# A chunked state-space scan on one core: its chunks taken in pairs, with two buffers each for B, inputs and decayed inputs

## The chip, the core and the metric

The kernel runs on one core of a Trainium2 chip. The metric is device time in microseconds (us) of one execution, the median of several; lower is better. The engines are TensorE (PE in the profile, with its weight loads as PEld), VectorE (DVE), ScalarE (ACT), GpSimd (POOL) and the queue engine SyncE (SP). Each engine takes its own instructions strictly in the order in which they were written down for it, and they wait for one another through semaphores.

## What is computed

One layer of a hybrid decoder in float32: a layer norm, a wide projection, a convolution branch (31 taps) beside a Mamba-2 state-space branch, a gated sum, an output projection, and a convolutional feed-forward part. The change touches only the chunked state-space scan. Cut to that, the reference is:

```python
# 1024 steps, chunks of L = 128; 4 groups g of 8 heads r, head size p = 64, state n = 128
a_cs  = cumsum(dt * a_head)                          # inside a chunk
decay = tril(exp(a_cs[l] - a_cs[s]))
cb     = einsum("bclgn,bcsgn->bcgls", C, B)
y_diag = einsum("bcgrls,bcsgrp->bclgrp", cb * decay, x * dt)
states = einsum("bclgn,bcgrl,bclgrp->bcgrpn", B, exp(a_cs[-1] - a_cs), x * dt)
carry  = exp(a_cs[-1]) * carry + states              # from chunk to chunk
y_off  = einsum("bclgn,bcgrpn,bcgrl->bclgrp", C, carry_before, exp(a_cs))
y      = y_diag + y_off
```

## The kernel before

The sequence is worked through in two halves of 512 steps (`hh` 0 and 1). In each half `mixers` runs four groups of heads (`g` 0 to 3). For a group it projects B, C and x (`column`, `conv4`) and the convolution branch (`glu`), calls `ssd_group`, which goes over the four chunks of 128 steps in that half, and then writes the 31-tap convolution `conv31` (30 VectorE instructions of 128x512 for each of two tiles) at low priority. `combine` follows: it reads the convolution back, averages over channels (the sum `mean` on POOL, its split `avgm`, and the matmul at L757), and multiplies with the next weights. The second half of the kernel is the feed-forward part, which the change does not touch.

Nearly all of TensorE's work is the split-precision projection `mm3` (L175, L176, L177): three 128x512 matmuls for each weight block. In the prediction "a projection matmul" is one of these. Every weight block is loaded by SP, rounded by ACT (L141) and its rest is formed by VectorE (L142) before TensorE can use it, in three rotating buffers.

For each chunk `ssd_group` has these parts:

- **transposes** of x and B (L570, L573) and the product of C and B (L574), into two PSUM banks (`px`, `pb`) of the four-bank pool "sm";
- a load of the cumulative sums `m` (L580, 512 KB, issued by POOL, two buffers), eight Relu (L585) and one Exp (L589) on ACT, and the masking product `m * cbm` (L601) on VectorE;
- `xs` (L593) on VectorE, the copy `bt` (L577) and the decayed inputs `xsd` (L600, eight instructions) on ACT;
- **carried** (L606): four matmuls of the state with C, and the product at L607;
- **masked** (L610): eight matmuls, one for each head. Each uses 64 of the array's 128 columns, even heads the lower and odd heads the upper half;
- **update** (L620): one 128x512 matmul that makes the new state. An explicit order keeps it behind the chunk's masked products (`tc.issue_after`, L619). L624 and L627 then update the state on VectorE, and L631 adds the masked products to the result.

Plain float32 matmuls (all of these) are two records each in the profile, the transposes one. `bt`, `xs` and `xsd` have one buffer. The order on each engine comes from a scheduler that lists instructions by priority, when its own timeline has their inputs ready; projections of later weights are put between the parts of a chunk.

Of the kernel before, what the change touches and what calls it, by code (L numbers as in the profile page):

```python
# [54 lines left out]
def kernel(  # L55
# [322 lines left out]
    def time_steps(pl, hh, ps):  # L378

        n2 = 2 * HEADS  # L380
        dtc = pl.tile([n2, HALF], F32, tag="yo", bufs=2, name=f"dtc{hh}")
        A.activation(
            out=dtc, in_=ps[:n2, :], func=AF.Identity, bias=pc[:n2, PC_DTB : PC_DTB + 1]
        )
        pt = bank(0)
        for c in range(4):
            TE.transpose(pt[:, c * n2 : (c + 1) * n2], dtc[:, c * P : (c + 1) * P], ident[:n2, :n2])
        n = 4 * HEADS
        dtv, wds = (d.rearrange("p c h -> p (c h)") for d in dts)
        work = pl.tile([P, 8 * P], F32, tag="m", bufs=2, name=f"sp{hh}")  # L390
        v, s, s2, q, a = (work[:, i * n : (i + 1) * n] for i in range(5))
        ea = work[:, 5 * n : 6 * n + HEADS]
        e = ea[:, :n]
        V.tensor_scalar_mul(ea[:, n:], a_log, -1.0)
        pv = pt[:, : 2 * n].rearrange("p (c i h) -> p c i h", c=4, i=2)
        vv = v.rearrange("p (c h) -> p c h", c=4)
        V.tensor_copy(vv, pv[:, :, 0, :])
        V.tensor_tensor(out=vv, in0=vv, in1=pv[:, :, 1, :], op=ALU.add)
        A.activation(out=e, in_=v, func=AF.Abs)
        A.activation(out=ea, in_=ea, func=AF.Exp, scale=-1.0)  # L400
        V.tensor_scalar_add(s, e, 2.0)
        V.reciprocal(out=s, in_=s)
        V.tensor_mul(s, s, e)
        V.tensor_mul(s2, s, s)
        V.tensor_scalar(
            out=q, in0=s2, scalar1=1.0 / 17.0, scalar2=1.0 / 15.0, op0=ALU.mult, op1=ALU.add
        )
        for k in (13, 11, 9, 7, 5, 3):
            V.tensor_mul(q, q, s2)
            V.tensor_scalar_add(q, q, 1.0 / k)  # L410
        V.tensor_mul(q, q, s2)
        V.scalar_tensor_tensor(out=q, in0=q, scalar=1.0, in1=s, op0=ALU.add, op1=ALU.mult)
        V.tensor_scalar_max(v, v, 0.0)
        V.scalar_tensor_tensor(out=dtv, in0=q, scalar=2.0, in1=v, op0=ALU.mult, op1=ALU.add)
        V.scalar_tensor_tensor(
            out=a.rearrange("p (c h) -> p c h", c=4),
            in0=dts[0],
            scalar=-1.0,
            in1=ea[:, n:].unsqueeze(1).to_broadcast([P, 4, HEADS]),
            op0=ALU.mult,  # L420
            op1=ALU.mult,
        )
        pa = bank(0)
        for c in range(4):
            hs = slice(c * HEADS, (c + 1) * HEADS)
            TE.matmul(pa[hs, :P], a[:, hs], upper, start=True, stop=True)
        eh = pl.tile([P, HALF], F32, tag="yo", bufs=2, name=f"sp_eh{hh}")[:, :P]
        cum = pl.tile([P, HALF], F32, tag="xsd", name=f"sp_cum{hh}")[:, :P]
        A.activation(out=eh, in_=pa[:, :P], func=AF.Exp)
        V.tensor_copy(cum, pa[:, :P])  # L430
        G.dma_start(cum_scr[hh].rearrange("c h l -> (c h) l"), cum)
        for c in range(4):
            G.dma_start(e_scr[hh][:, c * P : (c + 1) * P], eh[c * HEADS : (c + 1) * HEADS])
        pc_t = bank(0)
        TE.transpose(pc_t[:, :P], cum, ident)
        V.tensor_copy(cums.rearrange("p c h -> p (c h)"), pc_t[:, :n])
        pe = bank(0)
        for i, m in enumerate((later, ones)):
            TE.matmul(pe[:, i * n : (i + 1) * n], m, a, start=True, stop=True)
        ev = edc.rearrange("p i c h -> p (i c h)")  # L440
        A.activation(out=ev, in_=pe[:, : 2 * n], func=AF.Exp)
        V.tensor_mul(wds, dtv, edc[:, 0].rearrange("p c h -> p (c h)"))
# [103 lines left out]
    def ssd_group(pl, hh, g, xT, BT, CT, gate):  # L546
# [13 lines left out]
        def by_tile(t):  # L560
            return t.rearrange("p (i t) -> p i t", i=4)

        for c in range(4):
            nm = f"{hh}_{g}_{c}"
            cs = slice(c * P, (c + 1) * P)
            first = hh == 0 and c == 0
            last = hh == 1 and c == 3
            px = bank(0)
            for i in range(4):
# [2 lines left out]
            if not last:  # L572
                TE.transpose(pb[:, :P], BT[:, cs], ident)  # L573
            TE.matmul(pb[:, P : 2 * P], BT[:, cs], CT[:, cs], start=True, stop=True)  # L574
            if not last:
                bt = pl.tile([P, P], F32, tag="bt", name=f"bt{nm}")
                A.copy(bt, pb[:, :P])  # L577
            m = pl.tile([P, 8, P], F32, tag="m", bufs=2, name=f"m{nm}")
            mf = m.rearrange("p h l -> p (h l)")
# [9 lines left out]
            A.activation(out=mf, in_=mf, func=AF.Exp, scale=-1.0)  # L589
            cbm = pl.tile([P, P], F32, tag="cbm", name=f"cbm{nm}")  # L590
            V.tensor_mul(cbm, pb[:, P : 2 * P], upper)
            xs = pl.tile([P, HALF], F32, tag="xs", name=f"xs{nm}")
            V.tensor_tensor(  # L593
                out=heads(xs), in0=heads(px), in1=per_head(dts[0][:, c, h8]), op=ALU.mult
            )
            if not last:
                xsd = pl.tile([P, HALF], F32, tag="xsd", name=f"xsd{nm}")
                for h in range(8):
                    hs, k = slice(h * HP, (h + 1) * HP), 8 * g + h
                    A.mul(xsd[:, hs], px[:, hs], dts[1][:, c, k : k + 1])  # L600
            V.tensor_tensor(out=m, in0=m, in1=cbm.unsqueeze(1).to_broadcast([P, 8, P]), op=ALU.mult)  # L601
            if not first:
                po = bank(0)
                for i in range(4):
                    ts = slice(i * P, (i + 1) * P)
                    TE.matmul(po[:, ts], S[:, ts], CT[:, cs], start=True, stop=True)  # L606
                V.tensor_tensor(out=acc[:, :, cs], in0=by_tile(po), in1=acc[:, :, cs], op=ALU.mult)  # L607
            py = bank(0)
            for h in range(8):
                masked = TE.matmul(  # L610
                    py[h % 2 * HP : (h % 2 + 1) * HP, h // 2 * P : (h // 2 + 1) * P],
                    xs[:, h * HP : (h + 1) * HP],
                    m[:, h, :],
                    start=True,
                    stop=True,
                )
            if not last:
                pn = bank(0)
                with tc.issue_after(masked.ins):  # L619
                    TE.matmul(pn, bt, xsd, start=True, stop=True)  # L620
                if first:
                    V.tensor_copy(S, pn)
                else:
                    V.tensor_tensor(  # L624
                        out=heads(S), in0=heads(S), in1=per_head(edc[:, 1, c, h8]), op=ALU.mult
                    )
                    V.tensor_add(S, S, pn)  # L627
            if first:
                A.copy(acc[:, :, cs], by_tile(py))
            else:  # L630
                V.tensor_tensor(out=acc[:, :, cs], in0=acc[:, :, cs], in1=by_tile(py), op=ALU.add)  # L631
        zs = gate()
        ss = pl.tile([P, HALF], F32, tag="ss", name=f"ss{hh}_{g}")
        for i, y in enumerate(xT):
# [13 lines left out]
        def normed(yT):  # L648
            pm = bank(0)
            for c in range(4):  # L650
# [4 lines left out]
                    start=True,  # L655
                    stop=True,
                )
            r = pl.tile([P, P], F32, tag="rr", name=f"rr{hh}_{g}")
            A.activation(out=r, in_=pm[:, :P], func=AF.Sqrt, bias=eps, scale=1.0 / HALF)
            V.reciprocal(out=r, in_=r)  # L660
            rd = r_scr[hh][g]
# [746 lines left out]
```

## Time and profile before

| What | Value |
|---|---|
| Median of 3 runs | 1937.97 us (1936.03 to 1938.17) |
| The profiled execution | 1941.19 us, its span 1939.4 us |
| VectorE, ScalarE, GpSimd busy | 1631.4, 1112.9, 131.8 us |
| Chunks of the scan | 32 (2 halves, 4 groups, 4 chunks), between 79 and 1092 us |
| Mean granted TensorE clock | 0.998 |

The profiled execution took 3.2 us longer than the median of the runs. In a line of the timeline stand the start, the duration, engine, line, operation, output and inputs, shapes and the number of records merged into the line; in brackets the idle time before it and what ended it. A matmul is pipelined, so its duration reaches into the next one: the distance of two starts is what a matmul costs.

### The profile page before, as it was taken

The numbers are of one execution on the slowest core, as the hardware profiler recorded it, in microseconds if no ns is written. First come the engines' busy times: TensorE is split into PE (matmuls) and PEld (weight loads), VectorE is DVE, ScalarE is ACT, GpSimd is POOL, SyncE is SP. The second block draws the span as 40 slices with busy tenths as digits, with TensorE's granted clock in tenths as the row PEclk, the third lists the DMA queues.
The fourth block names the chain that finished last, engine by engine and source line by source line (L and its number), as shares of the span: only waits on it lengthen the run. The fifth ranks groups of instructions, "written<-read, shape, count | busy, mean of one in ns | idle before, by whom it ended". The sixth has DMA issues, their size and how long they took to land.

```text
span 1939.4 us, 24858 instructions
## 1 busy us (share of the span) xinstructions
PE 1912.4 (99%) x9106; PEld 1568.7 (81%) x9106; DVE 1631.4 (84%) x2215; ACT 1112.9 (57%) x1849; POOL 131.8 (7%) x184
## 2 busy tenths in 40 slices
PE   7999999999999999999999999999999999999998
PEld 6888888888788888888888888888888888888886
DVE  7699999898666889999999966588998887888768
ACT  6787878473453268777855445365655455453442
POOL 0100000000400010000000040001000000021000
PEclk9999999999999999999999999999999999999999
DMA  6434343524445643434353354576443322368572
GB/s 224 142 115 132 108 132 114 179 98 147 157 137 203 227 125 110 144 105 138 114 174 114 135 172 132 174 250 244 158 158 109 114 104 93 113 239 270 175 250 109
DMA packets 104010, 297.67 MB, mean 153 GB/s; under 512 B 12368, under 2 KB 12528, under 8 KB 103888
## 3 DMA queue, kind: packets, MB, share of 16 engines
q1 hardware_dynamic: 87840, 244.68, 37.4%
q0 software_dynamic: 13744, 47.21, 7.6%
q10 hardware_dynamic: 2304, 4.20, 0.6%
q8 instruction: 71, 1.16, 0.2%
q14 instruction: 51, 0.42, 0.1%
HBM read 246.22 MB, written 49.82 MB: 153 GB/s over the span
## 4 chain that ended last, share of the span: by engine, by line
PE 91%; DMA 3%; DVE 3%; ACT 1%; issue 1%; POOL 1%; SPq 0%; DVEq 0%; POOLq 0%; ACTq 0%
PE acc L175 24%; PE acc L176 24%; PE acc L177 24%; PE sm L175 3%; PE sm L176 3%; PE sm L177 3%; PE sm L610 2%; PE sm L620 2%; PE sm L606 1%; PE acc L328 1%; DMA st_wo<-wo 1%; PE sm L570 1%; DVE rows L239 1%; DMA m<-cum_scr 1%; DVE rows L242 0%
## 5 line engine op out<-in xcount | busy, mean ns | idle before, releaser
L522 DVE SCALAR_TENSOR_TENSOR c<-v,pc,c 128x512 f32<-128x512 f32 x480 | 342.6, 743 | 3.0 <-ACT c L511 1.9
L177 PE MATMUL acc<-hT,w_c 128*128 128x512 f32 x368 | 144.8, 394 | 0.0
L176 PE MATMUL acc<-hT,w_c 128*128 128x512 f32 x368 | 144.4, 392 | 0.0
L175 PE MATMUL acc<-hT,w_c 128*128 128x512 f32 x368 | 144.4, 392 | 0.0
L1043 DVE SCALAR_TENSOR_TENSOR fo<-u,pc,fo 128x1024 f32<-128x1024 f32 x88 | 111.4, 1289 | 0.0
L477 DVE SCALAR_TENSOR_TENSOR xbc<-u,pc,xbc 128x512 f32<-128x512 f32 x144 | 104.7, 742 | 1.1 <-ACT xbc L475 1.0
L177 PE MATMUL acc<-h1s,w_s 128*128 128x512 f32 x264 | 102.8, 389 | 0.0
L175 PE MATMUL acc<-h1s,w_s 128*128 128x512 f32 x264 | 102.7, 389 | 0.0
L176 PE MATMUL acc<-h1s,w_s 128*128 128x512 f32 x264 | 102.7, 389 | 0.0
L175 PE MATMUL acc<-hT,w_z 128*128 128x512 f32 x256 | 100.7, 393 | 0.0
L177 PE MATMUL acc<-hT,w_z 128*128 128x512 f32 x256 | 100.5, 393 | 0.0
L585 ACT ACTIVATE m<-m,cums 128x128 f32<-128x128 f32 x256 | 79.0, 393 | 37.5 <-DMA m<-cum_scr 31.2
L176 PE MATMUL acc<-hT,w_z 128*128 128x512 f32 x256 | 100.2, 391 | 0.0
L1183 ACT CAST w_dn<-dr 128x1024 fp32r<-128x1024 f32 (+1 forms) x73 | 60.9, 843 | 66.9 <-DVE dr L1113 37.4
L175 PEld LDWEIGHTS acc<-hT,w_c 128*128 128x128 f32 x368 | 69.2, 188 | 14.5 <-issue 0.6
L1184 DVE TENSOR_TENSOR w_dn<-dr,w_dn 128x1024 fp32r<-128x1024 f32 (+1 forms) x73 | 70.0, 967 | 12.7 <-ACT w_dn L1183 12.4
L177 PEld LDWEIGHTS acc<-hT,w_c 128*128 128x128 f32 x368 | 69.2, 188 | 14.2 <-issue 0.5
L176 PEld LDWEIGHTS acc<-hT,w_c 128*128 128x128 f32 x368 | 69.2, 188 | 13.8 <-issue 0.2
L175 PE MATMUL sm<-h1b,w_s 128*128 128x512 f32 x176 | 68.5, 389 | 0.0
L176 PE MATMUL sm<-h1b,w_s 128*128 128x512 f32 x176 | 68.5, 389 | 0.0
L177 PE MATMUL sm<-h1b,w_s 128*128 128x512 f32 x176 | 68.5, 389 | 0.0
L142 DVE TENSOR_TENSOR w_c<-st_c,w_c 128x1024 fp32r<-128x1024 f32 x46 | 55.9, 1216 | 12.8 <-ACT w_c L141 12.8
(384 smaller groups left out, 5554.7 us busy)
## 6 DMA issues: line engine op xcount, KB each, us to landing
st_c<-wcol SPq DMA_DIRECT2D x46, 512.0 KB, 3.4
st_z<-wz SPq DMA_DIRECT2D x32, 512.0 KB, 3.4
m<-cum_scr POOLq DMA_DIRECT2D x32, 512.0 KB, 4.6
st_wo<-wo SPq DMA_DIRECT2D x24, 512.0 KB, 4.0
ra<-wup SPq DMA_DIRECT2D x22, 512.0 KB, 3.6
rb<-wup SPq DMA_DIRECT2D x22, 512.0 KB, 3.2
t_scr<-fo POOLq DMA_DIRECT2D x22, 512.0 KB, 3.3
dr<-t_scr SPq DMA_DIRECT2D x44, 256.0 KB, 3.6
```

Source lines behind the costliest of these rows:

```text
L142: (eng or V).tensor_tensor(out=w[:, 1, :], in0=st, in1=w[:, 0, :].bitcast(F32), op=ALU.subtract)
L175: TE.matmul(ps, wa(0), xa(0), start=start, stop=False, skip_group_check=more)
L176: TE.matmul(ps, wa(0), xa(1), start=False, stop=False, skip_group_check=more)
L177: TE.matmul(ps, wa(1), xa(0), start=False, stop=stop, skip_group_check=more)
L477: V.scalar_tensor_tensor(out=o, in0=u[:, k : k + HALF], scalar=pc[:, wc + k : wc + k + 1], in1=o, op0=ALU.mult, op1=ALU.add,)
L522: V.scalar_tensor_tensor(out=accs[i], in0=v[:, k : k + HALF], scalar=pc[:, wc + k : wc + k + 1], in1=accs[i], op0=ALU.mult, op1=ALU.add,)
L585: A.activation(out=m[:, h, :], in_=m[:, h, :], func=AF.Relu, scale=-1.0, bias=cums[:, c, k : k + 1],)
L610: masked = TE.matmul(py[h % 2 * HP : (h % 2 + 1) * HP, h // 2 * P : (h // 2 + 1) * P], xs[:, h * HP : (h + 1) * HP], m[:, h, :], start=Tru ...
L620: TE.matmul(pn, bt, xsd, start=True, stop=True)
L1043: V.scalar_tensor_tensor(out=o, in0=u[:, k : k + T], scalar=pc[:, wc + k : wc + k + 1], in1=o, op0=ALU.mult, op1=ALU.add,)
L1183: A.copy(w[:, 0, cs], src)
L1184: V.tensor_tensor(out=w[:, 1, cs], in0=src, in1=w[:, 0, cs].bitcast(F32), op=ALU.subtract)
```

## The change

The loop over chunks becomes a loop over two pairs of chunks, (0, 1) and (2, 3). `chunk` prepares one chunk (transposes, `bt`, `m`, `xs`, `xsd`) and is called for both. Then the state goes ahead: carried and update of the first chunk, carried and update of the second. Last come the masked products of the second chunk and, tied behind them, those of the first. `bt`, `xs` and `xsd` get two buffers; the `r` of the group norm shares the buffers of `bt`. All instructions and shapes stay; one explicit order (update behind masked) goes, another (masked of the first behind masked of the second) comes.

```diff
-        for c in range(4):
+        def chunk(c):
...
             if not last:
-                bt = pl.tile([P, P], F32, tag="bt", name=f"bt{nm}")
+                bt = pl.tile([P, P], F32, tag="bt", bufs=2, name=f"bt{nm}")
...
-            xs = pl.tile([P, HALF], F32, tag="xs", name=f"xs{nm}")
+            xs = pl.tile([P, HALF], F32, tag="xs", bufs=2, name=f"xs{nm}")
...
-                xsd = pl.tile([P, HALF], F32, tag="xsd", name=f"xsd{nm}")
+                xsd = pl.tile([P, HALF], F32, tag="xsd", bufs=2, name=f"xsd{nm}")
...
+            return m, xs, bt, xsd
...
-            if not last:
-                pn = bank(0)
-                with tc.issue_after(masked.ins):
-                    TE.matmul(pn, bt, xsd, start=True, stop=True)
...
+        for c in (0, 2):
+            m0, xs0, *u0 = chunk(c)
+            m1, xs1, *u1 = chunk(c + 1)
+            carried(c)
+            update(c, *u0)
+            carried(c + 1)
+            update(c + 1, *u1)
+            py1, mm = masked(c + 1, m1, xs1)
+            with tc.issue_after(mm.ins):
+                py0, _ = masked(c, m0, xs0)
+            add(c + 1, py1)
+            add(c, py0)
...
-            r = pl.tile([P, P], F32, tag="rr", name=f"rr{hh}_{g}")
+            r = pl.tile([P, P], F32, tag="bt", bufs=2, name=f"rr{hh}_{g}")
```

In the changed file carried stands at L611, update at L618, masked at L630, the transposes at L569 and L572, the product of C and B at L573, and the averaging matmul at L783.

Three places show what the scheduler makes of it. The first is TensorE in group 0 of the first half. Before, each chunk's masked products stand alone between projections (`acc`), here those of chunk 0 (`m_0_0`), with the update and the next chunk's transposes behind them:

```order
L176 MATMUL acc_1046<-hT_187,w_z_0_1_1078 128x512
L610 MATMUL sm_867<-m_0_0_842,xs_0_0_855 64x128 x8
L620 MATMUL sm_876<-xsd_0_0_857,bt_0_0_840 128x512
L570 MATMUL sm_880<-ident,xbc_0_568 128x128
L570 MATMUL sm_880<-ident,xbc_1_608 128x128
L570 MATMUL sm_880<-ident,xbc_2_648 128x128
L570 MATMUL sm_880<-ident,xbc_3_688 128x128
L573 MATMUL sm_885<-ident,xbc_16_518 128x128
L574 MATMUL sm_885<-xbc_20_528,xbc_16_518 128x128
L177 MATMUL acc_1046<-hT_187,w_z_0_1_1078 128x512
```

With the change the masked products of chunks 1 and 0 are one run, behind carried and update:

```order
L177 MATMUL acc_1109<-hT_187,w_z_0_2_1113 128x512
L611 MATMUL sm_905<-xbc_20_528,state_112 128x128 x4
L618 MATMUL sm_911<-xsd_0_1_892,bt_0_1_875 128x512
L630 MATMUL sm_915<-m_0_1_877,xs_0_1_890 64x128 x8
L630 MATMUL sm_924<-m_0_0_842,xs_0_0_855 64x128 x8
L175 MATMUL acc_1109<-hT_187,w_z_0_2_1113 128x512
L176 MATMUL acc_1109<-hT_187,w_z_0_2_1113 128x512
L569 MATMUL sm_935<-ident,xbc_0_568 128x128
```

Over the whole kernel the 32 runs of eight masked products have become 16 runs of sixteen, with nothing inside any of them. Other small parts stand apart more often: interruptions of the projections that begin with a transpose, a carried or an update number 55 where there were 31.

The second place is ACT, in the same group: the work on `m` of chunk 2. Before, it stood one chunk ahead of its use, with one chunk's instructions:

```order
L542 ACTIVATE zs_0_1_1107<-acc_1046 128x512
L585 ACTIVATE m_0_2_945<-m_0_2_945,cums 128x128 x8
L600 ACTIVATE xsd_0_1_905<-sm_880,wds 128x64 x8
L589 ACT_TABLE_LOAD
L589 ACTIVATE m_0_2_945<-m_0_2_945 128x1024
L141 CAST w_c_37_1301<-st_c_37_1299 128x1024
```

Now chunks 2 and 3 are worked on together, between the masked run of chunks 0 and 1 and that of 2 and 3, and a weight (`w_c_20`) is rounded in their midst:

```order
L585 ACTIVATE m_0_2_945<-m_0_2_945,cums 128x128 x8
L600 ACTIVATE xsd_0_2_960<-sm_935,wds 128x64 x8
L585 ACTIVATE m_0_3_980<-m_0_3_980,cums 128x128 x4
L577 COPY bt_0_2_943<-sm_940 128x128
L589 ACT_TABLE_LOAD
L589 ACTIVATE m_0_2_945<-m_0_2_945 128x1024
L585 ACTIVATE m_0_3_980<-m_0_3_980,cums 128x128 x2
L577 COPY bt_0_3_978<-sm_975 128x128
L585 ACTIVATE m_0_3_980<-m_0_3_980,cums 128x128 x2
L600 ACTIVATE xsd_0_3_995<-sm_970,wds 128x64 x4
L141 CAST w_c_20_1341<-st_c_20_1339 128x1024
L600 ACTIVATE xsd_0_3_995<-sm_970,wds 128x64 x4
```

Behind these rows come a table load, the Silu of a `zs`, a table load and the Exp of `m_0_3`. In the whole order of ACT there are 106 table loads where there were 118.

The third place is TensorE in `combine` of the second half, where the averaging matmul takes `avgm`. Before:

```order
L177 MATMUL acc_9643<-hT_5211,w_gb_3_9646 128x512
L175 MATMUL acc_9677<-yT_2_8613,w_sp_2_9680 128x512
L176 MATMUL acc_9677<-yT_2_8613,w_sp_2_9680 128x512
L177 MATMUL acc_9677<-yT_2_8613,w_sp_2_9680 128x512
L757 MATMUL sm_10040<-avgm_10037,mean_w 128x512
```

With the change it stands inside the block of projections before:

```order
L177 MATMUL acc_9643<-hT_5211,w_gb_3_9646 128x512
L175 MATMUL acc_9643<-hT_5211,w_gb_3_9646 128x512
L176 MATMUL acc_9643<-hT_5211,w_gb_3_9646 128x512
L783 MATMUL sm_10040<-avgm_10037,mean_w 128x512
L177 MATMUL acc_9643<-hT_5211,w_gb_3_9646 128x512
```

Counted from the group norm's matmul (L651, now L677), 142 projection matmuls stand ahead of it instead of 153. In the first half it is 155 instead of 150.

More of the change, by code (lines that the diff above doesn't have):

```diff
@@ L427, in time_steps @@
         eh = pl.tile([P, HALF], F32, tag="yo", bufs=2, name=f"sp_eh{hh}")[:, :P]
-        cum = pl.tile([P, HALF], F32, tag="xsd", name=f"sp_cum{hh}")[:, :P]
+        cum = pl.tile([P, HALF], F32, tag="xsd", bufs=2, name=f"sp_cum{hh}")[:, :P]
         A.activation(out=eh, in_=pa[:, :P], func=AF.Exp)
@@ L561, in by_tile @@
             return t.rearrange("p (i t) -> p i t", i=4)
-        for c in range(4):
+        def chunk(c):
             nm = f"{hh}_{g}_{c}"
             cs = slice(c * P, (c + 1) * P)
-            first = hh == 0 and c == 0
             last = hh == 1 and c == 3
@@ L574, in ssd_group @@
             TE.matmul(pb[:, P : 2 * P], BT[:, cs], CT[:, cs], start=True, stop=True)
+            bt = xsd = None
             if not last:
-                bt = pl.tile([P, P], F32, tag="bt", name=f"bt{nm}")
+                bt = pl.tile([P, P], F32, tag="bt", bufs=2, name=f"bt{nm}")
                 A.copy(bt, pb[:, :P])
@@ L601, in ssd_group, with carried, update, masked @@
             V.tensor_tensor(out=m, in0=m, in1=cbm.unsqueeze(1).to_broadcast([P, 8, P]), op=ALU.mult)
[L602 to L607, printed above, removed]
+            return m, xs, bt, xsd
+        def carried(c):
+            if hh == 0 and c == 0:
+                return
+            cs = slice(c * P, (c + 1) * P)
+            po = bank(0)
+            for i in range(4):
+                ts = slice(i * P, (i + 1) * P)
+                TE.matmul(po[:, ts], S[:, ts], CT[:, cs], start=True, stop=True)
+            V.tensor_tensor(out=acc[:, :, cs], in0=by_tile(po), in1=acc[:, :, cs], op=ALU.mult)
+        def update(c, bt, xsd):
+            if hh == 1 and c == 3:
+                return
+            pn = bank(0)
+            TE.matmul(pn, bt, xsd, start=True, stop=True)
+            if hh == 0 and c == 0:
+                V.tensor_copy(S, pn)
+            else:
+                V.tensor_tensor(
+                    out=heads(S), in0=heads(S), in1=per_head(edc[:, 1, c, h8]), op=ALU.mult
+                )
+                V.tensor_add(S, S, pn)
+        def masked(c, m, xs):
             py = bank(0)
             for h in range(8):
-                masked = TE.matmul(
+                mm = TE.matmul(
                     py[h % 2 * HP : (h % 2 + 1) * HP, h // 2 * P : (h // 2 + 1) * P],
@@ L616, in ssd_group, with add @@
                 )
-            if not last:
-                pn = bank(0)
-                with tc.issue_after(masked.ins):
[L620 to L628, printed above, removed]
+            return py, mm
+        def add(c, py):
+            cs = slice(c * P, (c + 1) * P)
+            if hh == 0 and c == 0:
                 A.copy(acc[:, :, cs], by_tile(py))
```

## The prediction

> **What bounds the kernel.** I read the page's busy times first, then the busy time by stretches, then TensorE's waits.
>
> ```profile
> PE 1912.4 (99%) x9106; PEld 1568.7 (81%) x9106; DVE 1631.4 (84%) x2215; ACT 1112.9 (57%) x1849; POOL 131.8 (7%) x184
> 160.00:460.00 300.00, 300.00 (x1525) 242.53 (x1525) 286.48 (x404) 209.58 (x415) 11.53 (x20) 1.00 0.39 125
> PE sm L610 <- DVE m L601: 0.3, 1, 0.3
> 504.18 0.39 PE L177 MATMUL acc<-hT,w_gb 128*128 128x512 f32 x1
> ...
> 504.86 0.39 PE L177 MATMUL acc<-hT,w_gb 128*128 128x512 f32 x1
> ```
>
> TensorE is busy 99% of the span. In the stretch from 160 to 460 us, inside the first half's scan, it is busy for all 300.00 us, with VectorE at 286.48 and ACT at 209.58. Over all chunks TensorE waits once, for 0.3 us. So a chunk is worth what it takes from TensorE's issue, and VectorE, with 4.5% left, is the engine that could come next. Busy time hides what an instruction costs, because it overlaps; I take distances of starts. The last two rows, of the timeline, are three projection matmuls apart and 0.68 us: 0.227 a step.
>
> **What a masked run costs.** Four runs of before stand alone between projections. Here is one, and the line's own durations:
>
> ```profile
> 784.46 0.39 PE L177 MATMUL acc<-hT,w_c 128*128 128x512 f32 x1
> 784.78 1.09 PE L610 MATMUL sm<-m,xs 128*64 128x128 f32 x16
> 785.81 0.50 PE L175 MATMUL acc<-hT,w_c 128*128 128x512 f32 x1
> ...
> 787.07 0.39 PE L177 MATMUL acc<-hT,w_c 128*128 128x512 f32 x1
> L610 PE MATMUL sm<-m,xs x512: 272/273/324, 90.9 to 1090.1; 128*64 128x128 f32 x171
> ```
>
> From 784.46 to 787.07 are 2.61 us, with six projection steps in them (the last row is the sixth projection behind the run; 1.36 us), so the run costs 1.25 us. Its 16 records start within 1.09 - 0.27 = 0.82 us, 0.109 us a head; eight heads are 0.87 us. The other **0.38 us is paid for entering and leaving**: the first masked start comes 0.32 after a projection instead of 0.23, and the rest is paid on the way out. Is that paid by each run, whatever follows? A run with an update behind it:
>
> ```profile
> 445.94 0.39 PE L175 MATMUL acc<-hT,w_gt 128*128 128x512 f32 x1
> 446.26 1.09 PE L610 MATMUL sm<-m,xs 128*64 128x128 f32 x16
> 447.29 1.13 PE L620 MATMUL sm<-xsd,bt 128*128 128x512 f32 x2
> ...
> 449.41 0.40 PE L175 MATMUL acc<-hT,w_gt 128*128 128x512 f32 x1
> ```
>
> 3.47 us less six steps are 2.11 (the last row is again the sixth projection), so the update adds 0.86 us, and the toll was paid once. A full-width part between projections pays almost nothing:
>
> ```profile
> 98.70 0.39 PE L175 MATMUL acc<-hT,w_z 128*128 128x512 f32 x1
> 98.93 1.05 PE L606 MATMUL sm<-xbc,state 128*128 128x128 f32 x8
> ...
> 101.20 0.39 PE L176 MATMUL acc<-hT,w_z 128*128 128x512 f32 x1
> ```
>
> 2.50 us less seven steps (five more projections stand between) are 0.91 for eight records; they start 1.05 - 0.27 = 0.78 us apart over seven intervals, 0.111 each, so 0.89 of work and about 0.025 of toll.
>
> **The sum on TensorE.** The number of instructions stays. 32 masked runs become 16: 16 x 0.38 = **6.1 us less**. The order shows 24 more interruptions by full-width parts: 24 x 0.025 = 0.6 us more. Net **-5.5 us**. The trace has no update directly behind a projection. From the rows it costs 0.86, or more by whatever part of the toll belongs to it in truth; a part of 0.1 would bring back 28 x 0.1 = 2.8 us. The run without an update pays the whole toll too, so I take 0, and 2.8 as the other end. ACT saves 12 table loads of 1.28 us (row below), off the path.
>
> **What is tighter.** Both `m` buffers now come free at the end of a masked run, and both chunks' `m` must be loaded and worked on before the next. The rows of before:
>
> ```profile
> 65.05 1.25 POOL L552 DMA_DIRECT2D ys<-e_scr  x2 [1.25 <-PE acc L177]
> 66.29 9.84 DMA m<-cum_scr
> 92.55 0.54 POOL L580 DMA_DIRECT2D m<-cum_scr  x1 [25.13 <-DVE c L522]
> DMA to landing us min/median/max: 3.6/4.6/11.4
> 96.86 2.45 ACT L585 ACTIVATE m<-m,cums 128x128 f32<-128x128 f32 x8 [1.20 <-DMA m<-cum_scr]
> 99.83 1.75 ACT L600 ACTIVATE xsd<-sm,wds 128x64 f32<-128x64 f32 x8 [0.52 <-DVE xs L593]
> 101.60 1.28 ACT L589 ACT_TABLE_LOAD   x1
> 102.89 1.06 ACT L589 ACTIVATE m<-m 128x1024 f32<-128x1024 f32 x1
> 103.86 1.03 ACT L141 CAST w_c<-st_c 128x1024 fp32r<-128x1024 f32 x1
> 106.20 0.60 ACT L542 ACTIVATE zs<-acc 128x512 f32<-128x512 f32 x1
> 102.97 1.22 DVE L601 TENSOR_TENSOR m<-m,cbm 128x1024 f32<-128x1024 f32 x1
> ```
>
> Take the second pair of group 0, whose ACT rows the order shows. From the end of the masked run: POOL issues 0.5 us later, the first load lands after 4.6, so ACT starts at about 5.2. Two sets of Relu 4.9, two of `xsd` 3.5, three table loads 3.8, two Exp 2.1, a cast 1.0, a `zs` 0.6 and two small copies 0.5 (an estimate, a third of a cast each at most) make 16.4: done at 21.6, and with the masking product at 22.9. TensorE meanwhile has 86 projection matmuls (19.5 us), two carried (0.91, 0.89), two updates (0.89, 0.86) and 14 records of transposes and of C with B at 0.11 (1.6 with toll): it wants `m` at 24.7. **1.8 us to spare.** Counted in the same way, the tightest others of the eight second pairs are group 3 (0.7) and group 1 (3.5) of the first half; the rest have over 5 us. `w_c_20` is rounded at about 16.4 and ready on VectorE by 18.4; it is wanted at 20.4. I charge **+0.5 us** for all eight, 0 and 5 as the ends. VectorE's order was rebuilt but its work is the same; its 4.5% covers the 0.7 us a group that TensorE gains.
>
> **The averaging matmul.** Here the number of projections ahead of it changed.
>
> ```profile
> 470.59 0.43 PE L651 MATMUL sm<-ss,ones 128*32 128x128 f32 x8
> 507.66 0.50 PE L757 MATMUL sm<-avgm,mean_w 128*128 128x512 f32 x1 [2.41 <-ACT avgm L751]
> ...
> 512.32 0.39 PE L177 MATMUL acc<-hT,w_gb 128*128 128x512 f32 x1
> 500.00:540.00 40.00, 37.59 (x160) 30.61 (x159) 26.48 (x32) 20.06 (x26) 17.79 (x12) 0.96 0.38 126
> 1113.19 0.43 PE L651 MATMUL sm<-ss,ones 128*32 128x128 f32 x8
> 1148.39 0.50 PE L757 MATMUL sm<-avgm,mean_w 128*128 128x512 f32 x1
> 1147.71 0.62 ACT L751 CAST avgm<-mean 128x512 fp32r<-128x512 f32 x1 [4.22 <-POOL mean L763]
> ```
>
> From L651 until `avgm` is there pass 37.1 us in the first half and 35.2 in the second; that chain (norm, two small DMAs, the reload of `c`, seven sums on POOL) does not hang on TensorE. In the first half TensorE arrived early and lost 7.46 us less 14 steps (3.18), 4.3 us: 2.6 of wait, and 1.7 on a slower clock behind it: the granted clock of 500 to 540 us is 0.96 where 1.00 stands in the scan, and 0.04 of 40 us are 1.6. With 155 instead of 150 ahead the wait shrinks to about 1.5: I take 2 us gained (0 to 4.3). In the second half it arrived just in time; with 142 instead of 153 it is 2.5 us early, so 2.5 lost, less if the reload of `c`, which now has one weight load fewer in its midst, is 1 us sooner: I take 2 us lost (0 to 4.2, which is 2.5 and the 1.7 of clock). Net **0**.
>
> The Trainium skill, TensorE: Matmul & The Clock Gate, section Part 1: The HAM clock gate, has the clock halved only after an idle window of about 3.4 us; here a wait of 2.41 us already cost clock (0.96). By the page the second half could lose 2.5 at most and the end 4.2 above falls away; I kept it.
>
> Together -5.5 + 0.5 + 0 = **-5.0 us**. The profiled execution took 1941.19 us, 1.8 of it outside its span; it would come to 1936.2 (span 1934.4). It lies 3.2 us above the median of the runs, so I take the difference over: 1937.97 - 5.0 = **1933.0**.
>
> **Rivals.**
>
> 1. *The second pairs wait for `m`.* If the three tight places are late by 1.5 us each (other work in front of ACT or VectorE, which take theirs in order), 4.5 us return: 1937.5. For it: 0.7 us to spare in group 3. Against: ACT is 30% idle there, and in the row at 96.86 it waited 1.20 us for a load without TensorE noticing.
>
> 2. *Slower: two loads issued together land together, late.* The first `m` of a half took 9.84 us with a second issued behind it. If all pairs do, ACT is 5 us later at eight places, and behind its Relu stand weight casts. With 1.8, 3.5 and 0.7 to spare this costs 3.2 + 1.5 + 4.3 = 9.0 us: -5.0 + 9.0 = +4.0, 1942.0. It costs something from 5.3 us for a pair's first load (4.6 + 0.7) and has eaten the whole gain at about 8.3 (3.0 + 1.9 + 0.2). Against it: two loads of `ys`, 1 MB, were queued just ahead at 65.05. The Trainium skill, DMA: Bandwidth & Descriptors, section Anatomy of one DMA, fits 2.0 us plus bytes over 436 KB/us; by it two loads are there after 4.4 us, and this rival falls.
>
> 3. *More is gained.* Both waits for `avgm` vanish because the chain follows its new order, as the scheduler meant: -5.5 - 4.3 + 0.5 = -9.3, 1928.7.
>
> 4. *The change does not do what it says:* the toll is paid at each change of bank or of chunk inside a run, so 16 merged runs still cost 2 x 1.25 us each. Then only +0.6 and +0.5 remain: 1939.1. Against: in a run the halves of the array alternate eight times at 0.109.
>
> **How the numbers follow.** Forecast 0.55 (1930.5 to 1936; about 0.38 of it beyond 0.2%, which is 3.9 us and about what a measurement of this kernel can tell from no change); rival 1: 0.17; rival 2: 0.11; rival 3: 0.12; rival 4: 0.05. Faster: 0.38 + 0.12 = 0.50. Same: 0.17 + 0.17 + 0.05 = 0.39. Slower: 0.11. The range runs from 1928.5 (rival 3) to 1939.5 (rivals 1 and 4), which leaves out rival 2 and the tails.
>
> **What would show it.** In the new profile a masked run of 32 records should cost 2 x 0.87 + 0.38 = 2.1 us between projections, and an update alone 0.89. TensorE's waits should name `m` for under 1 us in all, and `avgm` for about 1.5 and 2.5 us. `m` loads issued together should land 4 to 6 us after issue. I am wrong if masked runs cost 2.5, if an update costs 1.0, or if TensorE waits for `m` or for weights at several second pairs.

## The result and the profile after

The changed kernel takes **1948.74 us** (median of 5 runs, 1947.13 to 1950.29) against 1937.97: the ratio is 1.0055, with a 95% interval of 1.0044 to 1.0066. It is 10.8 us slower, where 5 us faster was forecast. Its profiled execution took 1947.13 us (span 1945.4), the fastest of its five runs, while the profiled execution of before lay 3.2 us above its median. So the two traces show 5.9 us of the 10.8 between them; the other 4.9 lie in the spread of the executions, and no trace can place them.

First the views that answer to those of before: the busy times, the stretch from 160 to 460 us, and TensorE's waits (total in us, number, longest).

```profile
PE 1910.5 (98%) x9106; PEld 1570.7 (81%) x9106; DVE 1630.0 (84%) x2215; ACT 1094.3 (56%) x1837; POOL 135.0 (7%) x184
160.00:460.00 300.00, 298.13 (x1517) 242.45 (x1516) 280.69 (x394) 198.14 (x410) 11.52 (x20) 0.99 0.39 123
PE acc L175 <- ACT w_gg L141: 3.9, 2, 3.5
PE acc L175 <- ACT w_ga L141: 3.7, 2, 1.9
PE sm L618 <- ACT xsd L600: 1.9, 1, 1.9
PE acc L175 <- ACT w_so L141: 1.0, 1, 1.0
```

The engines have the work they had (ScalarE 18.6 us less, 15.4 of it the twelve table loads). What is new is that TensorE waits for weights: 8.6 us for `w_gg`, `w_ga` and `w_so`, none of which appear in the waits of before. All are weights of the next group of heads, wanted behind the masked run of a group's second pair. Two such passages, from group 0 to 1 and from 1 to 2 of the first half, before and then after (stretch, length, busy time of PE, PEld, DVE, ACT, POOL, granted clock, DMA share, GB/s):

```profile
122.00:160.00 38.00, 38.00 (x182) 31.02 (x181) 38.00 (x55) 32.82 (x68) 1.80 (x3) 1.00 0.50 144
222.00:260.00 38.00, 38.00 (x182) 31.03 (x181) 36.11 (x51) 34.57 (x66) 1.81 (x3) 1.00 0.41 125
```

```profile
122.00:160.00 38.00, 34.54 (x171) 27.80 (x170) 34.91 (x50) 30.25 (x57) 2.34 (x4) 0.96 0.50 146
222.00:260.00 38.00, 36.13 (x178) 29.11 (x177) 38.00 (x54) 30.95 (x59) 2.34 (x4) 0.96 0.45 141
```

TensorE loses 3.46 and 1.87 us to waiting, and clock on top (the granted clock is 0.96). These two windows serve for the experiments, too.

How does a weight come late? Here is ScalarE in the first of the passages, in its own order, with the issue of the load that it waits for (left out are the other three Relu of the first chunk, table loads, Silu, small copies, and the `u` and `xbc` of the convolutions):

```profile
124.96 1.05 ACT L141 CAST w_c<-st_c 128x1024 fp32r<-128x1024 f32 x1
...
129.86 0.54 POOL L580 DMA_DIRECT2D m<-cum_scr  x1 [25.97 <-PE sm L630]
...
134.88 1.58 ACT L585 ACTIVATE m<-m,cums 128x128 f32<-128x128 f32 x5 [7.63 <-DMA m<-cum_scr]
...
139.27 1.04 ACT L141 CAST w_c<-st_c 128x1024 fp32r<-128x1024 f32 x1
...
141.35 2.46 ACT L585 ACTIVATE m<-m,cums 128x128 f32<-128x128 f32 x8
...
145.12 1.06 ACT L589 ACTIVATE m<-m 128x1024 f32<-128x1024 f32 x1
...
148.20 1.03 ACT L141 CAST w_ga<-st_ga 128x1024 fp32r<-128x1024 f32 x1
...
151.69 1.06 ACT L589 ACTIVATE m<-m 128x1024 f32<-128x1024 f32 x1
152.74 1.04 ACT L141 CAST w_gg<-st_gg 128x1024 fp32r<-128x1024 f32 x1
```

The Relu of the *next* group's first chunk stand in ScalarE's queue ahead of the weight casts. They wait 7.63 us for their `m`, from 127.25 on: its buffer came free, and its load was issued, only when the first half of the merged run (128.46 to 130.43 us) was done. Everything behind them waits as well. Then come both chunks' Relu and Exp with their table loads, so that the four casts start 14.3, 8.9 and 4.5 us apart. A weight block lasts TensorE 24 x 0.227 = 5.4 us, and of three buffers two can be ahead. In before the same four casts start 10.6, 2.2 and 8.2 us apart (123.45, 134.04, 136.21, 144.36), with only one of the two `m` between the first and the third. The last two of them in before:

```profile
136.21 1.05 ACT L141 CAST w_ga<-st_ga 128x1024 fp32r<-128x1024 f32 x1
...
144.36 1.04 ACT L141 CAST w_gg<-st_gg 128x1024 fp32r<-128x1024 f32 x1
```

In the second of the passages the same block of two chunks' Relu and Exp stands among the casts, but what ScalarE waited for ahead of it was not a load:

```profile
235.23 0.73 ACT L487 ACTIVATE xbc<-xbc,pc 128x512 f32<-128x512 f32 x1 [6.28 <-DVE xbc L477]
```

Of the four longest waits of TensorE for a weight of the scan, ScalarE's longest wait ahead of the casts was for the load of an `m` in two (before the waits of 3.46 and 0.97 us) and for VectorE's `xbc` in the other two (before those of 1.87 and 1.85 us). The block of `m` work is in all four. TensorE in the first passage of the changed kernel:

```profile
149.98 0.39 PE L176 MATMUL acc<-hT,w_ga 128*128 128x512 f32 x1
153.83 0.50 PE L175 MATMUL acc<-hT,w_gg 128*128 128x512 f32 x1 [3.46 <-ACT w_gg L141]
...
155.01 0.63 PE L176 MATMUL acc<-hT,w_ga 128*128 128x512 f32 x1
```

It starts 1.1 us after the cast of `w_gg` has started. From 155.01 us on, seven matmuls come every 0.43 us, at half clock (granted clock from 150 to 159 us: 0.81).

I kept one **ledger** for all traces: between the first and the last of the 7716 projection matmuls, what lies beyond 0.2267 us a step, split into lateness (each gap beyond the median of its kind, and steps at half clock, that is of 0.43 us) and the rest, which is real work. Before: 146.3 us, of it 7.3 late. After: 152.6, of it 18.9 late. So the **work fell by some 5 us** (139.0 to 133.7) and the **lateness rose by 11.6**: 9.4 at weights, 3.7 of half clock behind them, 2.2 at the program's first update (`xsd` is late by ScalarE, at 90 us), 1.6 at small places; before's averaging wait and its clock, 4.3 us, went, and its other waits fell by 1.0.

### The profile page after: what moved, and what is told of

The parts are those of the page before. It is cut to its first block, busy times and chain, and to the rows that moved or that the text cites. A ratio compares the mean times of both kernels' runs of the same rounds, so it can differ in the third digit from the quotient of the medians.

```text
span 1945.4 us, 24844 instructions
## 1 busy us (share of the span) xinstructions
PE 1910.5 (98%) x9106; PEld 1570.7 (81%) x9106; DVE 1630.0 (84%) x2215; ACT 1094.3 (56%) x1837; POOL 135.0 (7%) x184
## 4 chain that ended last, share of the span: by engine, by line
PE 82%; ACT 6%; DVE 6%; DMA 3%; issue 2%; POOL 0%; SPq 0%; DVEq 0%; ACTq 0%; POOLq 0%
PE acc L175 22%; PE acc L176 22%; PE acc L177 22%; PE sm L177 3%; PE sm L175 3%; PE sm L176 3%; DMA m<-cum_scr 2%; ACT m L585 2%; DVE c L522 1%; PE sm L630 1%; PE sm L611 1%; PE sm L618 1%; PE acc L328 1%; ACT L589 1%; DMA st_wo<-wo 1%
## 5 line engine op out<-in xcount | busy, mean ns | idle before, releaser
L175 PE MATMUL acc<-hT,w_z 128*128 128x512 f32 x256 | 103.4, 404 | 0.0
L177 PE MATMUL acc<-hT,w_z 128*128 128x512 f32 x256 | 101.6, 397 | 0.0
L176 PE MATMUL acc<-hT,w_z 128*128 128x512 f32 x256 | 101.1, 395 | 0.0
L141 ACT CAST w_c<-st_c 128x1024 fp32r<-128x1024 f32 x46 | 49.0, 1065 | 54.4 <-issue 26.6
```

What stands on the lines that cost most here:

```text
L141: A.copy(w[:, 0, :], st)
L175: TE.matmul(ps, wa(0), xa(0), start=start, stop=False, skip_group_check=more)
L176: TE.matmul(ps, wa(0), xa(1), start=False, stop=False, skip_group_check=more)
L177: TE.matmul(ps, wa(1), xa(0), start=False, stop=stop, skip_group_check=more)
```

## The experiments

Theory 1: ScalarE's in-order queue, as just read. Theory 2: VectorE, whose part of the scan (state, sums) now comes bunched, holds `xbc`, and through ScalarE's queue the casts. Theory 3: it costs to prepare two chunks at once and put the updates ahead, not to merge the products. All times are medians of 4 to 11 executions, and each ratio is to executions of the kernel before that ran beside them (its medians lay between 1937.19 and 1938.27). A trace is of one execution, which lies up to 3.4 us from its median.

### Which merge costs

Merging undone for both pairs, then for the second pair only, then for the first only; the rest of the change stays. The first of them:

```diff
             update(c, *u0)
+            py0, _ = masked(c, m0, xs0)
+            add(c, py0)
             carried(c + 1)
             update(c + 1, *u1)
-            py1, mm = masked(c + 1, m1, xs1)
-            with tc.issue_after(mm.ins):
-                py0, _ = masked(c, m0, xs0)
+            py1, _ = masked(c + 1, m1, xs1)
             add(c + 1, py1)
-            add(c, py0)
```

> The changed kernel with its pairs, its second buffers and its updates ahead, but each chunk's masked product again a run of its own right behind that chunk's update: the first m buffer of a pair comes free a chunk earlier, and 16 tolls of 0.37 us return (+6 us of PE). Theory 1 (ScalarE's queue: both m of the next group's first pair are worked, after a late load, ahead of the weight casts): PE's waits for w_ga, w_gg and w_so shrink from 8.7 us to under 4, the halved-clock stretches behind 150 and 251 us go, and the time is 1940 (1936 to 1944). Theory 2 (VectorE's tail of the scan is bunched because the updates go ahead): as in the changed kernel plus the tolls, 1952 to 1956. Theory 3 (preparing two chunks at once is what costs): the same 1952 to 1956.

> Of each group only the first pair (chunks 0 and 1) has the merged masked run; the second pair's two products stand apart, each behind its update, so that the next group's m_0 can load a chunk earlier. Half of the tolls saved return (+3 us). Theory 1: the loss sits at the passage from one group to the next, which the second pair makes; it goes, and the time is 1937 (1934 to 1941). Theories 2 and 3: nothing of the loss goes, 1951 (1949 to 1954).

> The mirror of the run before: only the second pair (chunks 2 and 3) is merged. Theory 1: the loss at the passage to the next group stays and half of the tolls return, 1951 (1948 to 1954), 10 us or more above the kernel with only the first pair merged. Theories 2 and 3: as the kernel with only the first pair merged, within 3 us.

| Kernel | us | Ratio (95%) |
|---|---|---|
| none merged | 1941.64 | 1.0017 (1.0008 to 1.0025) |
| first pairs merged | 1939.54 | 1.0008 (0.9999 to 1.0017) |
| second pairs merged | 1947.9 | 1.0039 (1.0026 to 1.0052) |

All three fall on theory 1's side (the last is 0.1 below its range, and 8.4 above the kernel with first pairs merged where 10 were expected). The passage at 222 us, first with only first pairs merged, then with only second pairs:

```profile
222.00:260.00 38.00, 38.00 (x182) 31.01 (x181) 38.00 (x55) 30.75 (x56) 1.81 (x3) 1.00 0.47 141
```

```profile
222.00:260.00 38.00, 34.34 (x146) 27.77 (x143) 35.33 (x52) 28.00 (x52) 2.20 (x4) 0.91 0.46 138
```

Most of the loss is made by the second pair's merge. VectorE, full in the first of these windows (38.00), costs nothing there, which speaks against theory 2. But with none merged the kernel still stands 3.4 us above before, clear of the noise, so a smaller part comes with preparing pairs and with the updates ahead (theory 3). In its trace the first update waits 1.9 us, with some 1.6 us of half clock behind it.

### Moving the `m` work behind the casts

All products stay merged; an explicit order puts the Relu of a group's first two chunks behind a weight cast. First behind the last of the four glu weights:

```diff
-            A.copy(w[:, 0, :], st)
+            casts[name] = A.copy(w[:, 0, :], st)
...
-                A.activation(
...
+                behind = c < 2 and casts[f"gg{hh}_{2 * g + 1}"].ins
+                with tc.issue_after(behind) if behind else nullcontext():
+                    A.activation(
...
```

> The changed kernel with one thing added: the Relu passes of the first two chunks of a group are issued on ScalarE only behind the cast of the group's fourth glu weight, so that no weight cast of glu stands behind them. All products stay merged. Theory 1: the waits for w_ga and w_gg go (7.5 us, with some 9 us of halved clock that hang on them), 1935 (1931 to 1940), under the kernel before. Theory 2: VectorE is as late as it was, and holds xbc and the weights' second halves: 1946 to 1950. Theory 3: 1947 to 1951, with the masked runs of the first pair now waiting for m as well.

Measured 1947.69 us (1.0050, 1.0038 to 1.0062): a miss for theory 1. But the waits it speaks of are gone. TensorE's longest waits behind the start, and the stretch after the passage (the traced execution took 1951.04 us):

```profile
PE sm L575 <- ACT rr L690: 3.9, 2, 2.2
PE sm L623 <- ACT xsd L605: 3.4, 2, 2.3
PE sm L572 <- ACT xbc L490: 1.5, 2, 1.2
162.00:200.00 38.00, 35.12 (x154) 27.94 (x153) 29.83 (x42) 32.00 (x60) 1.19 (x2) 0.91 0.26 83
```

No weight of the scan is waited for; TensorE is now late at the chunk's transposes (`xbc`, and a PSUM bank that `rr` holds), one projection block further on. ScalarE's block of some 10 us (16 Relu 4.9, two Exp 2.1, two table loads 2.6) was not cured but moved. I took up **theory 4**: what costs is that block standing together wherever it stands. The next kernels were a third buffer for `m`, with a control that has only the smaller `zs` and `ya`, and the two chunks' work spread out, behind the first and the third glu weight (the edit above with `ga{hh}_{2 * g + c}`). The third buffer, cut:

```diff
...
-                z = pl.tile([P, HALF], F32, tag="zs", bufs=5, ...
+                z = pl.tile([P, HALF], F32, tag="zs", bufs=4, ...
...
-            m = pl.tile([P, 8, P], F32, tag="m", bufs=2, ...
+            m = pl.tile([P, 8, P], F32, tag="m", bufs=3, ...
...
-            y = pl.tile([P, HALF], F32, tag="ya", bufs=2, ...
+            y = pl.tile([P, HALF], F32, tag="ya", bufs=1, ...
...
```

> The control for the run with three m buffers: the changed kernel with four z gates in place of five and one output tile of the first SSM half in place of two, which frees 4 KB, and m still in two buffers. No theory sees these tiles in a wait that ends last: 1949 (1946 to 1952).

> The control with a third m buffer in the room that it frees: all products stay merged, but the next group's first m has a buffer that chunk 1's product freed long before, and its load, Relu and Exp come ahead of the weight casts without a wait. Theory 1 (a load that is late because a merged run frees both buffers at once, and ScalarE's order that waits for it ahead of the weight casts): the weight waits fall from 8.7 to under 3 us and the slow stretches behind them go, 1937 (1933 to 1941), 10 us or more under the control. Theory 2 (VectorE's backlog): as the control, within 3 us. Theory 4, which the run with both Relu passes behind the last glu weight suggests (there the weight waits went and as much came back where ScalarE was late for the next pair's transposes): what costs is ScalarE's 10 us of m work standing together, wherever it stands; then three buffers, which put another m there, gain less than 4 us on the control.

> The changed kernel, all products merged, with the Relu passes of a group's chunk 0 issued on ScalarE behind the cast of the group's first glu weight, and those of chunk 1 behind the third: the waiting for the load goes, and the two blocks of m work stand apart, 11 us from each other. Theory 1 in its narrow form (the wait for the late load): 1938 (1934 to 1942). Theory 4 (the 10 us together are too much): the same, since they are apart; told from theory 1 by the run with both behind the fourth weight, where the load had long landed and the time was 1947.7. Theory 2 (VectorE): 1946 to 1950.

The control: 1948.98 (1.0056, 1.0043 to 1.0069). Three buffers: **1951.07** (1.0063, 1.0051 to 1.0076), no gain. Spread: **1940.3** (1.0007, 0.9998 to 1.0017), 8.4 us under the changed kernel. With three buffers the next group's first `m` is early, but the scheduler uses the room to put chunk 2's `m` into the same stretch as well, and ScalarE waits for VectorE's `xbc` ahead of the casts (4.7 us in two waits before `w_ga`, the longer one below); the weights stay late:

```profile
139.76 0.72 ACT L487 ACTIVATE xbc<-xbc,pc 128x512 f32<-128x512 f32 x1 [2.94 <-DVE xbc L477]
```

So a third buffer, and with it an early load, is not enough. As other `m` work moved into its place, an early load by itself stays untried. With the work spread, the two windows and ScalarE's order in the first are:

```profile
122.00:160.00 38.00, 38.00 (x195) 31.16 (x194) 37.22 (x54) 31.06 (x60) 2.34 (x4) 1.00 0.50 159
222.00:260.00 38.00, 37.38 (x190) 30.32 (x189) 38.00 (x53) 31.07 (x59) 2.34 (x4) 1.00 0.50 151
```

```profile
140.91 1.06 ACT L144 CAST w_ga<-st_ga 128x1024 fp32r<-128x1024 f32 x1 [0.17 <-PE acc L180]
...
143.00 2.46 ACT L590 ACTIVATE m<-m,cums 128x128 f32<-128x128 f32 x8
...
147.82 1.03 ACT L144 CAST w_gg<-st_gg 128x1024 fp32r<-128x1024 f32 x1
```

`w_ga` is cast at 140.91 instead of 148.20 and `w_gg` at 147.82 instead of 152.74, with the same instructions. No Relu waits for its load in this passage. In the second passage ScalarE waits for VectorE's `xbc` no less than in the changed kernel (6.80 us, up to 233.19, against 6.28), and yet TensorE waits only 0.62 us for a weight there. So what VectorE does to ScalarE's queue does not cost much where the two chunks' `m` work is not one block behind it.

### VectorE or ScalarE

Two pairs of kernels, each the kernel before and the changed one with the same work left out. First every second of the 31 taps of the convolution on VectorE (`range(0, KC - 1, 2)`):

> The kernel before with 15 of the 30 taps of the 31-tap convolution left out on VectorE (some 145 of its 1630 us); everything else stands. It is the base for the next run; VectorE is not what the end waits for in the kernel before: all theories 1925 to 1938.

> The changed kernel with the same 15 taps left out, to be read against the run before it; with all taps the distance is +10.8. Theory 2 (VectorE's backlog holds xbc, and through ScalarE's queue the casts): VectorE has the slack to catch up, and the changed kernel stands 2 to 7 us under its base. Theories 1 and 4 (ScalarE's queue, whatever VectorE does): it stands 7 to 12 us above it.

Measured 1938.67 (1.0003, 0.9994 to 1.0011) and 1946.33 (1.0038, 1.0026 to 1.0051): 7.7 us apart. The number is theories 1 and 4's, the reason is not. The changed kernel's first passage and its main waits:

```profile
122.00:160.00 38.00, 38.00 (x199) 30.77 (x199) 31.68 (x43) 35.76 (x67) 3.54 (x6) 1.00 0.51 153
PE sm L569 <- DVE ys L612: 2.4, 4, 1.2
PE sm L630 <- DVE m L601: 2.1, 2, 1.5
PE sm L618 <- ACT xsd L600: 1.9, 1, 1.9
```

The weights are in time, so VectorE's lag has its share in their lateness; but the scheduler packed the scan differently, and TensorE waits inside it instead. What this pair shows is that relief of VectorE doesn't bring the gain; it doesn't part VectorE's share from ScalarE's.

Then ScalarE's block itself made 3 us shorter, with one Relu pass over all heads, which leaves out the other seven heads' own bias:

```diff
-            for h in range(8):
-                k = 8 * g + h
-                A.activation(
-                    out=m[:, h, :], in_=m[:, h, :], func=AF.Relu, scale=-1.0,
-                    bias=cums[:, c, k : k + 1],
-                )
+            A.activation(
+                out=mf, in_=mf, func=AF.Relu, scale=-1.0, bias=cums[:, c, 8 * g : 8 * g + 1]
+            )
```

> The kernel before with the eight Relu passes of a chunk replaced by one over all eight heads with the first head's bias (the other heads' values are left wrong): ScalarE has 1.5 us less per chunk, some 46 us in all. The base for the next run: 1932 to 1939 by all theories.

> The changed kernel with the same single Relu pass, to be read against the run before it. Theory 4 (ScalarE's 10 us block of m work in front of the weight casts is too long): the block is 3 us shorter and the distance falls from +10.8 to between -3 and +5. Theory 1 in its narrow form (the wait for the late load, not the work behind it): the wait stays, +6 to +11. Theory 2 (VectorE): +7 to +12.

Measured 1937.4 (0.9994, 0.9985 to 1.0003) and **1935.32** (0.9985, 0.9976 to 0.9995): the distance turns from +10.8 to -2.1. The shorter block takes the loss away; the kernel before hardly notices it. That the sign turns is less sure, as the two intervals overlap. In the changed kernel TensorE still waits for two weights of the scan, 1.8 us for `w_gg` and 0.2 for `w_ga`.

### Where the rest of the gain is

With the `m` work spread the changed kernel still stood 2 us above before. Its ledger names the first update (2.2 us at 90 us, and clock behind it), and other waits of updates for `xsd` and `bt`. Three kernels: with only first pairs merged, the very first pair in the order of before (`old_order`, not shown: of each chunk carried, masked, update); the same start with the `m` work spread; and with that, the second update of each pair behind the merged run. Last, the spread rule on the kernel before.

```diff
+            if hh == 0 and g == 0 and c == 0:
+                old_order(c, (m0, xs0, *u0), (m1, xs1, *u1))
+                continue
             carried(c)
             update(c, *u0)
```

> The kernel in which only first pairs are merged (1939.5), with the very first pair of the program, chunks 0 and 1 of group 0, in the order of before: each product first, its update behind it. There PE waited 1.9 us at 90 us for ScalarE's xsd with the update ahead, and ran at half clock for eight matmuls behind it, 3.8 us in all, which no other place shows. If the update put ahead of the product is the cause of that wait: it goes, one toll of 0.37 returns, and the time is 1936.0 (1934.5 to 1938), below the kernel before. If the wait comes from preparing two chunks at once instead: 1939 to 1941.

> The changed kernel with the m work of a group's first two chunks spread (behind the first and the third glu cast, 1940.3 alone), and the very first pair in the order of before. With the spread alone PE still waits 2.2 us for xsd at 90 us and is slow behind it; with only first pairs merged the old start took off 0.4 in the medians and 3.7 between the profiled spans. If that wait is the rest: 1936.5 (1935 to 1938), 0.1% under the kernel before. If other waits of the updates take it up: 1939 to 1941.

> The run before it, with the update of each pair's second chunk issued behind the merged products and not ahead of them, so that bt and xsd of that chunk have 2.1 us longer. If the updates put ahead cost in several places (waits for xsd and bt of 3.6 us in all with the spread): 1 to 3 us under the run before it. If they don't: within 1 us of it, or above, where a run of full-width matmuls more is paid at each pair (16 at 0.03).

> The kernel before with the same rule: the Relu passes of a group's chunk 0 behind the cast of its first glu weight, those of chunk 1 behind the third. It has its two m worked apart already, so by theory 4 the rule moves little: 1937 to 1940. If it stands 3 us or more under before, the recovery of the changed kernel with this rule was not a matter of the change.

The first: 1939.14 (1.0003, 0.9995 to 1.0012), which its interval can't tell from 1939.54, although the wait at 90 us is gone; a miss. So what that wait costs in the medians stays open. With the spread: 1937.43 (0.9998, 0.9989 to 1.0007), level with before. The update behind: 1942.9 (1.0029, 1.0017 to 1.0040), worse, so the updates do belong ahead; in its trace TensorE waits 2.0 us for the state at L616. The kernel before with the rule: 1937.08 (0.9999, 0.9990 to 1.0008), so the recovery is the changed kernel's own.

Last, `xsd` taken off ScalarE: one GpSimd operation per chunk in place of eight ScalarE passes, which makes the same `xsd` from `xs`.

```diff
-                for h in range(8):
-                    hs, k = slice(h * HP, (h + 1) * HP), 8 * g + h
-                    A.mul(xsd[:, hs], px[:, hs], dts[1][:, c, k : k + 1])
+                G.tensor_tensor(
+                    out=heads(xsd), in0=heads(xs), in1=per_head(edc[:, 0, c, h8]), op=ALU.mult
+                )
```

> The changed kernel with xsd made by one GpSimd operation per chunk (xs times the decay) in place of eight ScalarE passes: ScalarE has 1.7 us less per chunk, 54 us in all, but none of it in the block of Relu and Exp that stands ahead of the glu casts. Theory 4: the wait at 90 us (1.9, and 1.7 of half clock) goes, and the weight waits at the group passages fall by a part only: 1944 (1940 to 1947). If ScalarE's total load counts and not the block: 1936 to 1940.

> The kernel with the m work spread and the old start (1937.4), with xsd on GpSimd as well. If the waits left there are ScalarE's bursts: its waits for xsd and bt go, some 3 us with what hangs on them, 1934.5 (1933 to 1936.5), under both kernels. If GpSimd's order (it issues the loads of m too, and the product with xs would stand ahead of them) makes m late, or the updates wait for it: 1938 to 1943.

> The kernel before with xsd on GpSimd: no wait for xsd stands in its trace, so 1937 (1935 to 1939) by every theory; if it falls under 1935, ScalarE's relief is worth something to either kernel and the run before this one says nothing about the change.

The changed kernel with this alone: **1957.47** (1.0099, 1.0085 to 1.0113), 8.7 us slower still; no theory had it, and the wait at the first update didn't go: TensorE stands there 1.9 us for `bt`. With the spread and the old start: **1934.47** (0.9983, 0.9974 to 0.9992), the lowest median of all, as expected. The kernel before with it: 1936.61 (0.9995, 0.9986 to 1.0004). Busy times and waits of the first two:

```profile
PE 1915.6 (98%) x9106; PEld 1575.0 (81%) x9106; DVE 1645.6 (84%) x2215; ACT 1048.7 (54%) x1612; POOL 175.6 (9%) x212
PE acc L175 <- ACT w_gg L141: 5.2, 2, 3.4
PE acc L175 <- ACT w_so L141: 4.8, 2, 2.7
PE acc L175 <- ACT w_ga L141: 4.0, 2, 3.4
```

```profile
PE 1906.1 (99%) x9106; PEld 1569.8 (81%) x9106; DVE 1646.3 (85%) x2215; ACT 1045.2 (54%) x1609; POOL 175.3 (9%) x212
PE sm L623 <- DVE cbm L596: 1.1, 1, 1.1
PE sm L635 <- DVE m L606: 1.1, 1, 1.1
```

This pair says it best. ScalarE has the same load in both (1048.7 and 1045.2 us, 46 to 49 less than in the changed kernel), and they lie 23 us apart. With 46 us of work less, the waits for weights rose from 8.6 to 14.0. At the longest of them, 3.43 us for `w_gg` at 245.70 us, ScalarE had idled 4.94 us ahead of a `w_c` and 1.98 us ahead of 16 Relu in one piece; then 8.9 us of work stood between the casts of `w_ga` (235.67) and `w_gg` (244.61). It is the order that decides here, not the load.

## Why the prediction was wrong

- **The toll of a masked run, and the sum on TensorE: right.** A merged run between projections, and an update alone, in the changed kernel:

```profile
778.56 0.39 PE L177 MATMUL acc<-hT,w_c 128*128 128x512 f32 x1
778.88 1.97 PE L630 MATMUL sm<-m,xs 128*64 128x128 f32 x32
...
782.04 0.39 PE L177 MATMUL acc<-hT,w_c 128*128 128x512 f32 x1
...
116.68 0.39 PE L176 MATMUL acc<-hT,w_c 128*128 128x512 f32 x1
116.91 1.02 PE L618 MATMUL sm<-xsd,bt 128*128 128x512 f32 x2
...
118.68 0.39 PE L175 MATMUL acc<-hT,w_c 128*128 128x512 f32 x1
```

  3.48 us less six steps are 2.12 (2.1 predicted), and 2.00 less five steps 0.87 (0.89). The ledger's work fell by 5.3 us where 5.5 was forecast. Rival 4 is out.

- **"What is tighter": here it failed.** The step asked whether `m` would be ready for the *next masked run*, for the eight second pairs, and looked at one cast, `w_c_20`. That question had a good answer: over all chunks no wait for `m` reaches the list above. It didn't ask what stands behind the Relu at the passage to the next group. There the two `m` come free within 0.9 us of each other, so that their 16 Relu and two Exp stand as one block among the casts of the group's first weights; in the first passage their first load was issued (129.86) 2.6 us after ScalarE had come to the Relu (127.25). The charge of 0.5 us should have been 9.4 of weight waits and 3.7 of half clock. Against such waits rival 1 set that ScalarE is 30% idle; but its idle time lay in waits of its own order (7.63 us in the first passage), with the casts behind them.

- **Rival 2** had the right victim (weight casts behind the Relu) and the wrong cause: loads that land together after 8.3 us or more. The pair at 129.86 and 130.74 us, issue to landing:

```profile
DMA to landing us min/median/max: 4.9/5.3/5.6
```

  That is within the 4 to 6 us predicted. All `m` loads of the changed kernel landed after 3.7 to 6.7 us, except the first two of each half (8.6 to 11.4, in before 8.7 to 11.4). The load was late because it was issued late.

- **The updates ahead** were priced by TensorE's time alone. The program's first one waits 1.9 us for `xsd`, whose sixteen passes for two chunks now end together; this term was missing.

- **The averaging matmul**: net 0 predicted, 4 us gained in the profiled execution. The matmul that takes `avgm` first follows the projection ahead of it by 0.25 us at most (first and second half):

```profile
514.72 0.50 PE L783 MATMUL sm<-avgm,mean_w 128*128 128x512 f32 x1
1153.30 0.40 PE L783 MATMUL sm<-avgm,mean_w 128*128 128x512 f32 x1
```

  As rival 3 had it, the chain followed its new order: from the group norm's matmul it took 35.7 and 32.7 us, where it had taken 37.1 and 35.2. Whether the medians gained it, too, stays open: the profiled execution of before was 3.2 us above its median.

With the failing step mended the forecast mechanism pays, but not in full: 1935.32 against 1937.4 with the shorter block, 1934.47 against 1936.61 with `xsd` on GpSimd (and the spread and the old start in the changed kernel). That is 2 us of the 5, and in both pairs the intervals overlap a little. In the last pair the ledger has the other 3: 5.8 us late in the changed kernel against 2.9, in single waits of an update, of a masked run and of a chunk's transposes. That these are the price of two chunks' work coming at once on VectorE and ScalarE was not tried by itself.

## What to carry to other kernels

Merging work on the engine that bounds the kernel also merges what frees its buffers; ask, for each engine that must refill them, what stands *behind* the refill in its queue, for the next stage as well as for this one. Busy share says little about an engine that works strictly in order: an instruction that waits, for a late load or for another engine, delays unrelated work behind it, and a long block of work delays it further; the cure is where the block stands in the order. A schedule that is fixed in advance should be moved by explicit order at the few places where a load is late, in doses: here both blocks behind the last cast gained 1 us, one behind the first and one behind the third 8.4 us.

## What was not expected of the hardware

Waits that are nearly the same cost the clock or don't. TensorE in the changed kernel, at two waits for `w_ga`:

```profile
253.41 0.61 PE L175 MATMUL acc<-hT,w_ga 128*128 128x512 f32 x1 [1.87 <-ACT w_ga L141]
...
800.37 0.50 PE L175 MATMUL acc<-hT,w_ga 128*128 128x512 f32 x1 [1.85 <-ACT w_ga L141]
```

Behind the 1.87 us the steps are 0.43 us for nine matmuls (1.7 us more; the granted clock is 0.76 from 251 to 258 us), behind the 1.85 they stay at 0.23 (1.00 from 797 to 803 us). The first update is such a place, too: 1.91 us of wait in the changed kernel left the clock at 1.00 (88 to 94 us), 1.94 us in the kernel with only first pairs merged left it at 0.79 (89 to 97 us). The Trainium skill, TensorE: Matmul & The Clock Gate, section Part 1: The HAM clock gate, has the clock halved after at least one idle window of about 3.4 us, and has that window run free. That it runs free would fit two equal waits with unequal ends; that the clock goes after 1.87 us of wait, well under a window, does not fit its figure, and the measurement decides.
